# All scale rows before the first projections, head 0's values between the image's and the context's projections

## The chip, the cores and the metric

The kernel runs on one core of a Trainium2 chip. What counts is the device time of one execution in microseconds (us). Each core has TensorE (PE in the rows: matmuls), VectorE (DVE), ScalarE (ACT), GpSimd (POOL) and SyncE (SP, which here issues the loads). Each engine runs its instructions in the order in which the program hands them over, and waits where an instruction needs something of another engine.

## The reference, cut to what matters

One layer of a hybrid block: an adaptive norm, one input projection that feeds a retention mixer (4 heads) and an RG-LRU, their merge, and then an expert layer. The opening, with which this case deals, computes this:

```python
mod_x = silu(c) @ mod_w + mod_b          # shift and scale for the 512 image tokens
mod_c = silu(c_ctx) @ mod_w + mod_b      # the same for the 256 context tokens
hx = rms_norm(x, norm1_g) * (1 + scale_x) + shift_x
hc = rms_norm(ctx, norm1_g) * (1 + scale_c) + shift_c
px, pc = hx @ w_in, hc @ w_in            # parts: q, k, v (retention), gate, u, g (RG-LRU), ...
ux = short_conv(u_x); uc = short_conv(u_c)
r, i = sigmoid(ux @ wa + ba), sigmoid(ux @ wx + bx)   # RG-LRU gates, blocks of 128 channels
h[t] = a[t] * h[t-1] + sqrt(1 - a[t]**2) * i[t] * u[t]  # scan over tokens, both directions; a from r
```

A head of the retention takes scores q k^T with a decay mask, times v, context tokens first; v of a head has 256 columns.

## The kernel before

Everything is kept with the 1024 channels in 8 tiles (KT) of 128 partitions, the tokens along the free axis: 512 of the image (NX), 256 of the context (NC_), 768 together (NT). float32 products are made of three matmuls (mm3, lines 64 to 67): each operand is split into a high part h and a low part l (split, lines 60 to 62: ScalarE copies the high part, VectorE subtracts to get the low one), and hi x hi, hi x lo and lo x hi are added.

The opening: SP loads the inputs. VectorE and ScalarE sum the squares of xT (the image, inv_rms, lines 174 to 186); a matmul with ones spreads the sum (ps_ss), a VectorE instruction scales it and adds epsilon, ScalarE takes the root, VectorE the reciprocal (rstd). Shift and scale of channel tile k come in one of two ways: for k < 4 (NROW) by matmuls, "mod rows" (mod_rows1, lines 198 to 207: 16 matmul instructions on TensorE for image and context at once, a copy by ScalarE, two transposes, two small VectorE instructions); for k of 4 to 7 by two dot products on VectorE for the image (s=0) and two for the context (s=1) (mod_dots, lines 210 to 216). normed (lines 218 to 223) then makes hh and hl (image) or ch and cl (context) of one tile: VectorE, ScalarE, VectorE. The weights of the mod rows (mw, 1 MB each) have two buffers, those of the dot products (mwc, 1 MB each) four; projection weights (w, 512 KB) are loaded in the order of the list plan, two buffers for the loads and four for the split tiles.

The loop over KORD = (0, 4, 1, 2, 5, 6, 3, 7) brings one tile after another: mod rows 2 and 3 or the dot products, normed, then the tile's part of four projections into the PSUM tiles pu, p5, pk and pq (outs0). The context's dot products, norm and projections (into columns 512 to 767 of pu and pk) are written behind it.

Then the loop over four heads. For each: lru_in makes the convolved u from pu (ScalarE copy u, line 303, then six VectorE taps, line 310; split into uh and ul) and the gelu g5 from p5; head computes masks, ropes of k and q, the values v (a PSUM tile pv for two of six token tiles, 24 matmuls for each token tile; vm is the mean, vh and vl the split), then for six tiles scores pS, the masked product P (split to Ph and Pl) and po. lru_scan makes the four gates pg by matmuls from uh and ul (line 65 to 67, 24 in all), then ScalarE and VectorE steps (roots, gi, a, q) and scans (lines 353 to 357). A head has two LRU blocks c = 2h and 2h + 1; the second one's pu and p5 are projected in between.

PSUM has three buffers of 1024 columns (pu, pk, pg, po ..., tag ps2) and two of 512 (p5, pq, pS, pv, tag ps1). In which order each engine gets the instructions around there is set by a scheduler that lists them by its own estimate of when each could run. So the order in the code is not the order on the engines.

Of the kernel before, what the change touches and what calls it, by code (L numbers as in the profile page):

```python
# [17 lines left out]
OP = mybir.AluOpType  # L18
# [34 lines left out]
def block_kernel(ctx: ExitStack, tc: tile.TileContext, A):  # L53
# [10 lines left out]
    def mm3(out, wh, wl, xh, xl, start, stop):  # L64
        PE.matmul(out, wh, xh, start=start, stop=False)  # L65
        PE.matmul(out, wh, xl, start=False, stop=False)  # L66
        PE.matmul(out, wl, xh, start=False, stop=stop)  # L67
# [64 lines left out]
    for j, nm in enumerate(("c", "c_ctx")):  # L132
        S.activation(scol[:, :, j], col(nm, 0, 8), AF.Tanh, scale=0.5)
        V.tensor_scalar(scol[:, :, j], scol[:, :, j], 1.0, 0.5, op0=OP.add, op1=OP.mult)
        V.tensor_tensor(scol[:, :, j], scol[:, :, j], col(nm, 0, 8), op=OP.mult)
    mod1 = const.tile([128, KT, 2, 2], F32, name="mod1")
# [35 lines left out]
    rstd = st.tile([128, NT], F32, name="rstd")  # L172

    def inv_rms(src, o, n):
        ps = psum(n if n == NX else D, name="ps_ss")
        ssq = st.tile([128, NX], F32, name="ssq")
        S.activation(ssq[:, :n], src[:, 0], AF.Square)
        for k in range(1, KT):
            sq = st.tile([128, NX], F32, name="sq", bufs=2)
# [38 lines left out]
    def normed(src, n, s, k, h_, l_):  # L218
        xn = st.tile([128, NX], F32, name="xn", bufs=2)
# [3 lines left out]
        V.scalar_tensor_tensor(l_[:, k], xn[:, :n], shift, f(h_[:, k]), op0=OP.add, op1=OP.subtract)  # L223
# [21 lines left out]
    spin = const.tile([128, 24], F32, name="spin")  # L245
# [808 lines left out]
```

## Time and profile before

| | us |
|---|---|
| median of 3 runs | 1880.65 (1879.25 to 1881.04) |
| profiled execution | 1879.51 |
| its span in the trace | 1877.7 |
| first projection matmul starts | 30.50 |
| last image projection, first matmul behind it | 67.19 |
| first gate matmul | 82.53 |
| first score matmul pS | 115.31 |

In the rows a timeline line is: start, duration, engine, line of the kernel, operation, output <- inputs, shape, count; in brackets the engine's idle time just before and what ended it. Matmuls overlap, so the distance of two starts, not the duration, is what one costs. In a table by stage each engine has its busy time and, in brackets, its instructions. PEclk is the TensorE clock that was granted: 1.00 is 2.4 GHz, 0.50 is 1.2 GHz.

### The profile page before, as it was taken

The numbers are of one execution on the slowest core, as the hardware profiler recorded it, in microseconds if no ns is written. First come the engines' busy times: TensorE is split into PE (matmuls) and PEld (weight loads), VectorE is DVE, ScalarE is ACT, GpSimd is POOL, SyncE is SP. The second block draws the span as 40 slices with busy tenths as digits, with TensorE's granted clock in tenths as the row PEclk, the third lists the DMA queues.
The fourth block names the chain that finished last, engine by engine and source line by source line (L and its number), as shares of the span: only waits on it lengthen the run. The fifth ranks groups of instructions, "written<-read, shape, count | busy, mean of one in ns | idle before, by whom it ended". The sixth has DMA issues, their size and how long they took to land.

```text
span 1877.7 us, 26999 instructions
## 1 busy us (share of the span) xinstructions
PE 1820.2 (97%) x9969; PEld 1603.0 (85%) x9969; DVE 1512.3 (81%) x2801; ACT 824.3 (44%) x1213; POOL 375.7 (20%) x327
## 2 busy tenths in 40 slices
PE   7899999999999999999999999999999999999997
PEld 3788888887888989999999988888887888888885
DVE  8987878788844579999988578886786879788688
ACT  4667575765222444445545333333333333333333
POOL 0000000000000000000022134443443535445350
PEclk9999999999999999999999999999999999999999
DMA  7122121225943433567778999998989999999986
GB/s 310 52 67 68 57 68 57 68 64 189 335 136 115 138 108 115 184 193 238 261 283 299 317 345 328 345 336 298 323 324 312 346 340 337 347 331 355 319 302 208
DMA packets 175753, 432.72 MB, mean 230 GB/s; under 512 B 14082, under 2 KB 87170, under 8 KB 171140
## 3 DMA queue, kind: packets, MB, share of 16 engines
q1 hardware_dynamic: 138756, 296.75, 46.7%
q0 software_dynamic: 36864, 134.23, 19.7%
q8 instruction: 78, 1.28, 0.3%
q14 instruction: 55, 0.45, 0.1%
HBM read 389.32 MB, written 41.62 MB: 229 GB/s over the span
## 4 chain that ended last, share of the span: by engine, by line
PE 74%; DVE 11%; DMA 9%; ACT 3%; issue 2%; SPq 1%; DVEq 0%; ACTq 0%
PE po L65 8%; PE po L66 8%; PE po L67 8%; PE pS L65 7%; PE pS L66 7%; PE pS L67 7%; DMA wt<-wd 4%; DMA vw<-in_v_dram 2%; DVE wl L62 2%; PE pgm L65 1%; PE pgm L66 1%; PE pgm L67 1%; PE pmm L66 1%; PE pmm L67 1%; PE pmm L65 1%
## 5 line engine op out<-in xcount | busy, mean ns | idle before, releaser
L61 ACT ACTIVATE wh<-w 128x1024 fp32r<-128x1024 f32 (+1 forms) x216 | 224.8, 1043 | 369.0 <-DMA w<-in_uT_dram 105.0
L65 PE MATMUL pS<-h2h,wh 128*128 128x384 f32 x1024 | 347.1, 339 | 7.0 <-ACT gt L756 6.7
L67 PE MATMUL pS<-h2h,wl 128*128 128x384 f32 x1024 | 346.1, 338 | 0.7 <-DVE wl L62 0.7
L66 PE MATMUL pS<-h2l,wh 128*128 128x384 f32 x1024 | 346.2, 338 | 0.0
L62 DVE TENSOR_TENSOR wl<-w,wh 128x1024 fp32r<-128x1024 f32 (+1 forms) x216 | 259.0, 1200 | 88.2 <-ACT wh L61 87.5
L801 POOL DMA_INDIRECT row<-in_u_dram,ei x128 | 181.9, 1421 | 609.7 <-DVE row L803 316.0
L66 PE MATMUL po<-vwl,ah 128*128 128x512 f32 x768 | 299.9, 391 | 1.2 <-DVE vwl L62 1.2
L67 PE MATMUL po<-vwh,al 128*128 128x512 f32 x768 | 298.9, 390 | 0.0
L65 PE MATMUL po<-vwh,ah 128*128 128x512 f32 x768 | 271.5, 395 | 10.0 <-ACT vwh L61 8.1
L61 ACT ACTIVATE ah<-af 128x384 fp32r<-128x384 f32 x128 | 67.2, 525 | 387.0 <-PE po L66 220.2
L809 POOL DMA_INDIRECT row<-in_v_dram,ei x128 | 183.9, 1436 | 208.5 <-DVE acc L814 175.2
L65 PEld LDWEIGHTS pS<-h2h,wh 128*128 128x128 f32 x1024 | 193.2, 189 | 14.3 <-ACT gt L756 8.4
L67 PEld LDWEIGHTS pS<-h2h,wl 128*128 128x128 f32 x1024 | 193.1, 189 | 6.0 <-DVE wl L62 1.0
L66 PEld LDWEIGHTS pS<-h2l,wh 128*128 128x128 f32 x1024 | 193.3, 189 | 4.3
L62 DVE TENSOR_TENSOR vwl<-vw,vwh 128x1024 fp32r<-128x1024 f32 x128 | 156.1, 1220 | 27.1 <-ACT vwh L61 25.6
L65 PEld LDWEIGHTS po<-vwh,ah 128*128 128x128 f32 x768 | 143.1, 188 | 38.4 <-ACT vwh L61 10.6
L814 DVE SCALAR_TENSOR_TENSOR acc<-row,act,acc 128x1024 f32<-128x1024 f32 x127 | 162.7, 1281 | 14.0 <-DMA row<-in_v_dram,ei 13.4
L66 PEld LDWEIGHTS po<-vwl,ah 128*128 128x128 f32 x768 | 144.4, 188 | 29.9 <-DVE vwl L62 2.3
L67 PEld LDWEIGHTS po<-vwh,al 128*128 128x128 f32 x768 | 144.4, 188 | 27.8 <-DVE al L62 0.2
L61 ACT ACTIVATE vwh<-vw 128x1024 fp32r<-128x1024 f32 x128 | 134.4, 1051 | 61.6 <-DMA vw<-in_v_dram 59.9
L803 DVE SCALAR_TENSOR_TENSOR row<-row,h2t 128x1024 f32<-128x1024 f32 x128 | 153.8, 1220 | 2.4 <-DMA row<-in_u_dram,ei 2.4
L62 DVE TENSOR_TENSOR al<-af,ah 128x384 fp32r<-128x384 f32 x128 | 71.0, 554 | 62.6 <-ACT ah L61 57.5
(372 smaller groups left out, 3505.8 us busy)
## 6 DMA issues: line engine op xcount, KB each, us to landing
w<-in_uT_dram SPq DMA_DIRECT2D x128, 512.0 KB
vw<-in_v_dram SPq DMA_DIRECT2D x128, 512.0 KB
w<-in_w_in_dram SPq DMA_DIRECT2D x48, 512.0 KB
wd<-stg SPq DMA_DIRECT2D x24, 1024.0 KB
modb<-in_mod_t_dram SPq DMA_DIRECT2D x32, 512.0 KB
wt<-wd SPq DMA_DIRECT2D x9, 1536.0 KB
gd<-gt SPq DMA_DIRECT2D x57, 192.0 KB
gr<-gd SPq DMA_DIRECT2D x57, 192.0 KB
```

The costliest lines, as they stand in the source:

```text
L61: S.activation(hi, src, AF.Copy)
L62: V.tensor_tensor(lo, src, f(hi), op=OP.subtract)
L65: PE.matmul(out, wh, xh, start=start, stop=False)
L66: PE.matmul(out, wh, xl, start=False, stop=False)
L67: PE.matmul(out, wl, xh, start=False, stop=stop)
L801: G.indirect_dma_start(out=row, out_offset=None, in_=A["u"], in_offset=bass.IndirectOffsetOnAxis(ap=ei[:, j:j + 1], axis=0))
L803: V.scalar_tensor_tensor(row, row, 1.0, h2t, op0=OP.mult, op1=OP.mult, accum_out=act[:, j:j + 1])
L809: G.indirect_dma_start(out=row, out_offset=None, in_=A["v"], in_offset=bass.IndirectOffsetOnAxis(ap=ei[:, j:j + 1], axis=0))
L814: V.scalar_tensor_tensor(acc, row, act[:, j:j + 1], acc, op0=OP.mult, op1=OP.add)
```

## The change

The softplus constants (spin, sp and what follows) are written ahead of mod1 and c2, so ahead of the norm. The root is taken by ScalarE straight from PSUM. All four mod rows are written ahead of the projections (issue_after holds the projections back until the last row's transpose), in parts of the PSUM tiles that are used later: halves of pv0, and the free columns of pk and pu. The tiles are taken in the order 0 to 7, tiles 4 and 5 have their dot products before. The value weights of head 0 are loaded early. Behind the image's projections stand the image's values of head 0 (token tiles 0 to 3, into pv0), then the context's part: dot products, norm, projections, and its two value tiles into columns 768 to 1023 of pk and pu. In head(h) only heads 1 to 3 compute their values there; head 0 reads them from pv0 and pvc. In head 0 the step that splits the values stands before lru_scan.

```diff
@@ plan of the weight loads
-                 A["w_v"][h, :, 0:4], A["w_v"][h, :, 4:8], A["w_in"][17 + c], A["w_in"][25 + c], A["gate_w"][c + 1],
+                 *([A["w_v"][h, :, 0:4], A["w_v"][h, :, 4:8]] if h else []),
+                 A["w_in"][17 + c], A["w_in"][25 + c], A["gate_w"][c + 1],
...
@@ block_kernel, inv_rms and the opening
-    def inv_rms(src, o, n):
-        ps = psum(n if n == NX else D, name="ps_ss")
+    def inv_rms(src, o, ps):
+        n = src.shape[2]
...
-        PE.matmul(ps[:, :n], onesf, ssq[:, :n], start=True, stop=True)
-        r = rstd[:, o:o + n]
-        V.tensor_scalar(r, ps[:, :n], 1.0 / D, EPS, op0=OP.mult, op1=OP.add)
-        S.activation(r, r, AF.Sqrt)
-        V.reciprocal(r, r)
+        PE.matmul(ps, onesf, ssq[:, :n], start=True, stop=True)
+        S.activation(rstd[:, o:o + n], ps, AF.Sqrt, scale=1.0 / D, bias=epsc)
+        V.reciprocal(rstd[:, o:o + n], rstd[:, o:o + n])
...
-    inv_rms(xT, 0, NX)
-    KORD = (0, 4, 1, 2, 5, 6, 3, 7)
-    mws = {0: mod_load(0)}
-    prefetch(2)
-    prefetch(4)
-    for k in KORD[1:]:
-        mws[k] = mod_load(k)
-    first = [ahead.pop(0) for _ in range(4)]
-    for k in range(2):
-        mod_rows1(k, mws[k], psum(name="pr"))
-    outs0 = [psum(n, name=nm) for nm, n in (("pu", NT), ("p5", NX), ("pk", NT), ("pq", NX))]
-    for k in KORD:
-        if 1 < k < NROW:
-            mod_rows1(k, mws[k], psum(D, name="pr"))
-        elif k >= NROW:
-            mod_dots(k, mws[k], 0)
-        normed(xT, NX, 0, k, hh, hl)
-        for out, (wh, wl) in zip(outs0, first):
-            mm3(out[:, :NX], wh[:, k], wl[:, k], hh[:, k], hl[:, k], k == KORD[0], k == KORD[-1])
...
-    for k in range(NROW, KT):
-        mod_dots(k, mws[k], 1)
+    outs0 = [psum(n, name=nm) for nm, n in (("pu", NT), ("p5", NX), ("pk", NT), ("pq", NX))]
+    pv0 = psum(D, name="pv0")
+    inv_rms(xT, 0, outs0[1])
+    KORD = tuple(range(KT))
+    mws = {}
+    for k in (0, 4, 1, 5):
+        mws[k] = mod_load(k)
+    prefetch(2)
+    prs = pv0[:, :512], pv0[:, 512:], outs0[2][:, 512:], outs0[0][:, 512:]
+    for k in range(2):
+        mod_rows1(k, mws[k], prs[k])
+    for k in (2, 3, 6):
+        mws[k] = mod_load(k)
+    prefetch(4)
+    mws[7] = mod_load(7)
+    for k in (2, 3):
+        rows = mod_rows1(k, mws[k], prs[k])
     SY.dma_start(cT, A["cT"])
-    inv_rms(cT, NX, NC_)
-    for k in range(KT):
-        normed(cT, NC_, 1, k, ch, cl)
+    first = [ahead.pop(0) for _ in range(4)]
+    wv0 = []
+    for i in range(2):
+        w = wst.tile([128, 4, 256], F32, name="w", tag="w")
+        SY.dma_start(w, A["w_v"][0, :, 4 * i:4 * i + 4])
+        wv0.append([st.tile([128, 4, 256], F32R, name=f"wv{m}", bufs=2) for m in "hl"])
+        split(*wv0[i], w)
+    for k in (4, 5):
+        mod_dots(k, mws[k], 0)
+    with tc.issue_after(rows.ins):
+        for k in KORD:
+            if k > 5:
+                mod_dots(k, mws[k], 0)
+            x_done = normed(xT, NX, 0, k, hh, hl)
+            for out, (wh, wl) in zip(outs0, first):
+                mm = mm3(out[:, :NX], wh[:, k], wl[:, k], hh[:, k], hl[:, k], k == KORD[0], k == KORD[-1])
+
+    def values(out, t, wv):
+        th, tl, o = (hh, hl, 128 * t) if t < 4 else (ch, cl, 128 * t - NX)
+        for k in range(KT):
+            mm = mm3(out, th[:, k, o:o + 128], tl[:, k, o:o + 128], wv[k // 4][0][:, k % 4], wv[k // 4][1][:, k % 4], k == 0, k == KT - 1)
+        return mm
+
+    with tc.issue_after(x_done.ins):
+        inv_rms(cT, NX, outs0[0][:, NT:])
+
+    for t in range(4):
+        with tc.issue_after(mm.ins):
+            mm = values(pv0[:, 256 * t:256 * t + 256], t, wv0)
+    with tc.issue_after(x_done.ins):
+        for k in KORD:
+            if k >= NROW:
+                mod_dots(k, mws[k], 1)
+            normed(cT, NC_, 1, k, ch, cl)
+            for i in (0, 2):
+                wh, wl = first[i]
+                mm = mm3(outs0[i][:, NX:NT], wh[:, k], wl[:, k], ch[:, k], cl[:, k], k == 0, k == KT - 1)
+    pvc = [outs0[i][:, NT:] for i in (2, 0)]
+    for t in (4, 5):
+        with tc.issue_after(mm.ins):
+            mm = values(pvc[t - 4], t, wv0)
...
@@ head(h)
-        wv = [wtile() for i in range(2)]
+        wv = [wtile() for i in range(2)] if h else None
...
@@ loop over heads
             if h == 0:
                 pu, pp, pk, pq = outs0
-                proj_ctx(pu, *first[0])
                 li = lru_in(0, pu, pp)
-                proj_ctx(pk, *first[2])
...
             hd.send((pk, pq))
+            if h == 0:
+                next(hd)
             lru_scan(2 * h, *li)
-            next(hd)
+            if h:
+                next(hd)
```

The queue of loads on SP at the start, kernel before (mw are the tiles of the mod rows, in order 0 to 3; xT the image; m_116 the context cT):

```order
L171 DMA xT<-in_xT_dram 128x2048 x2
L192 DMA mw<-in_mod_a_dram 128x2048
L86 DMA w<-in_w_in_dram 128x1024 x2
L195 DMA mwc<-in_mod_c_dram 128x2048
L192 DMA mw<-in_mod_a_dram 128x2048
L195 DMA mwc<-in_mod_c_dram 128x2048 x3
L247 DMA spin<-in_rd_dram 128x8
L281 DMA m_116<-in_cT_dram 128x2048
L86 DMA w<-in_w_in_dram 128x1024 x2
L192 DMA mw<-in_mod_a_dram 128x2048 x2
```

The same queue in the changed kernel (m_161 is the context):

```order
L204 DMA xT<-in_xT_dram 128x2048 x2
L225 DMA mw<-in_mod_a_dram 128x2048
L228 DMA mwc<-in_mod_c_dram 128x2048
L225 DMA mw<-in_mod_a_dram 128x2048
L228 DMA mwc<-in_mod_c_dram 128x2048
L86 DMA w<-in_w_in_dram 128x1024 x2
L228 DMA mwc<-in_mod_c_dram 128x2048 x2
L275 DMA m_161<-in_cT_dram 128x2048
L225 DMA mw<-in_mod_a_dram 128x2048 x2
L86 DMA w<-in_w_in_dram 128x1024 x2
```

The third and fourth mod tile now stand before the second pair of projection weights, but still behind ten megabytes of other loads.

VectorE between the split of u and the second value tile's low part, kernel before (vm is the value tiles' mean, vl their low part, ul the low part of u, rt and kl the rope of k, sc a mask):

```order
L421 TENSOR_REDUCE vm<-pv 128x2
L389 TENSOR_TENSOR dt_566<-dt_566,dt_567 128x128
L422 TENSOR_SCALAR vm<-vm 128x2
L62 TENSOR_TENSOR ul<-u,uh 128x768
L397 TENSOR_TENSOR sc<-sc,dt_575 128x320
L426 SCALAR_TENSOR_TENSOR vl<-pv,vm,vh 128x256
L397 TENSOR_TENSOR sc<-sc,dt_581 128x320
L367 TENSOR_TENSOR rt<-rx,ssin 64x512 x2
L62 TENSOR_TENSOR kl<-pk,kh 128x256
L426 SCALAR_TENSOR_TENSOR vl<-pv,vm,vh 128x256
```

VectorE at the same place in the changed kernel, from the split of u to the low part of token tile 3 (pv_180 is pv0):

```order
L62 TENSOR_TENSOR ul<-u,uh 128x768
L457 TENSOR_REDUCE vm<-pu 128x1
L458 TENSOR_SCALAR vm<-vm 128x2
L353 SCALAR_TENSOR_TENSOR g_798<-g_798,x_796 128x512
L62 TENSOR_TENSOR wl<-w,wh 128x1024
L429 TENSOR_TENSOR sc<-sc,dt_772 128x320
L462 SCALAR_TENSOR_TENSOR vl<-pv_180,vm,vh 128x256
L429 TENSOR_TENSOR sc<-sc,dt_778 128x320
L399 TENSOR_TENSOR rt<-rx,ssin 64x512 x2
L62 TENSOR_TENSOR kl<-pk,kh 128x256
L457 TENSOR_REDUCE vm<-pk 128x1
L462 SCALAR_TENSOR_TENSOR vl<-pv_180,vm,vh 128x256
```

The low parts of tiles 2 and 3 now stand in the place of those of tiles 0 and 1, which have moved ahead of ul, between the taps.

VectorE behind the first scores, kernel before (P is the masked score, Pl its low part, ul the split of the second LRU block's u):

```order
L437 TENSOR_TENSOR P<-pS,sx 128x512
L62 TENSOR_TENSOR wl<-w,wh 128x1024
L62 TENSOR_TENSOR ul<-u,uh 128x768
L437 TENSOR_TENSOR P<-pS,sx 128x512
L318 TENSOR_SCALAR g_1036<-g_1036 128x512
L62 TENSOR_TENSOR Pl<-P,Ph 128x512
```

VectorE there in the changed kernel (gi<-a,gi are scans of the first LRU block, u taps of the second):

```order
L473 TENSOR_TENSOR P<-pS,sx 128x512
L385 SCALAR_TENSOR_TENSOR gi<-a,gi 128x256
L473 TENSOR_TENSOR P<-pS,sx 128x512
L62 TENSOR_TENSOR wl<-w,wh 128x1024
L389 SCALAR_TENSOR_TENSOR gi<-a,gi 128x768
L342 SCALAR_TENSOR_TENSOR u<-pu,cols,u 128x510
L342 SCALAR_TENSOR_TENSOR u<-pu,cols,u 128x254
L386 SCALAR_TENSOR_TENSOR gi<-a,gi 128x512
L62 TENSOR_TENSOR Pl<-P,Ph 128x512 x2
```

The scans and the first taps now stand between the first P and its low part.

## Rows read from the trace of the kernel before

**Rows 1.** The page, part 1: busy time, share of the span, instructions.

```profile
PE 1820.2 (97%) x9969; PEld 1603.0 (85%) x9969; DVE 1512.3 (81%) x2801; ACT 824.3 (44%) x1213; POOL 375.7 (20%) x327
```

**Rows 2.** Table by stage: stretch, length, busy time of each engine, clock, DMA.

```profile
30.50:67.19 36.69, 34.09 (x134) 22.88 (x135) 35.91 (x98) 16.46 (x30) 0.00 (x0) 0.91 0.25 96
...
79.60:90.00 10.40, 7.58 (x26) 5.89 (x26) 9.45 (x20) 8.61 (x15) 0.80 (x2) 0.67 0.09 25
...
115.30:135.00 19.70, 18.85 (x87) 14.97 (x86) 15.57 (x22) 18.72 (x24) 0.00 (x0) 1.00 0.18 54
135.00:200.00 65.00, 65.00 (x382) 57.49 (x381) 50.42 (x68) 37.03 (x51) 1.81 (x4) 1.00 0.15 49
```

**Rows 3.** Timeline of TensorE, start to the second half of the projections.

```profile
16.36 9.15 PE L200 MATMUL pr<-mw,scol 128*2 128x256 f32 x32
...
25.98 0.28 PE L204 MATMUL pr<-ident,row 2*128 2x2 f32 x2 [0.25 <-ACT row L202]
30.50 0.52 PE L65 MATMUL pu<-hh,wh 128*128 128x512 f32 x1 [4.24 <-ACT hh L222]
...
35.01 0.63 PE L66 MATMUL pu<-hl,wh 128*128 128x512 f32 x1
...
39.56 3.62 PE L200 MATMUL pr<-mw,scol 128*2 128x256 f32 x16
```

**Rows 4.** Timeline of TensorE, from the first gate to the first score.

```profile
82.53 1.22 PE L65 MATMUL pg<-uh,wh 128*128 128x512 f32 x2 [2.82 <-ACT uh L61]
...
89.99 0.28 PE L65 MATMUL pv<-wh,hh 128*128 128x256 f32 x1
...
101.50 0.40 PE L65 MATMUL pu<-hh,wh 128*128 128x512 f32 x1
...
109.84 0.40 PE L65 MATMUL p<-hh,wh 128*128 128x512 f32 x1
...
115.31 0.39 PE L65 MATMUL pS<-qh,kh 128*128 128x512 f32 x1
```

**Rows 5.** DMA from 0 to 36 us: GB/s in 40 slices, then the sum.

```profile
GB/s 0 3 165 100 373 382 419 428 419 428 428 419 391 428 451 423 437 419 428 419 419 437 428 391 437 428 419 419 357 120 301 374 378 410 442 437 441 423 410 428
DMA packets 2390, 13.37 MB, mean 371 GB/s; under 512 B 384, under 2 KB 512, under 8 KB 1026
```

**Rows 6.** Timeline of VectorE: one dot product of 16.

```profile
24.02 1.22 DVE L214 SCALAR_TENSOR_TENSOR mscr<-mwc,m 128x1024 f32<-128x1024 f32 x1
```

**Rows 7.** Timeline of ScalarE: the copy u.

```profile
74.38 0.98 ACT L303 ACTIVATE u<-pu,cols 128x768 f32<-128x768 f32 x1
```

**Rows 8.** Timeline of VectorE, from the taps to the second vl.

```profile
75.13 0.42 DVE L318 TENSOR_SCALAR g<-g 128x512 f32<-128x512 f32 x1
75.46 1.13 DVE L310 SCALAR_TENSOR_TENSOR u<-pu,cols,u 128x510 f32<-128x510 f32 x2
...
81.46 0.68 DVE L421 TENSOR_REDUCE vm<-pv 128x2 f32<-128x512 f32 x1
...
84.93 0.49 DVE L397 TENSOR_TENSOR sc<-sc,dt 128x320 f32<-128x320 f32 x1 [0.66 <-ACT sc L396]
...
87.22 0.47 DVE L426 SCALAR_TENSOR_TENSOR vl<-pv,vm,vh 128x256 fp32r<-128x256 f32 x1
```

**Rows 9.** Timeline of VectorE: scans of the first LRU block, first scores.

```profile
104.08 0.68 DVE L353 TENSOR_TENSOR_SCAN gi<-a,gi 128x256 f32<-128x256 f32 x1
...
105.79 1.75 DVE L357 TENSOR_TENSOR_SCAN gi<-a,gi 128x768 f32<-128x768 f32 x1
...
107.51 1.28 DVE L354 TENSOR_TENSOR_SCAN gi<-a,gi 128x512 f32<-128x512 f32 x1
...
116.19 0.69 DVE L437 TENSOR_TENSOR P<-pS,sx 128x512 f32<-128x512 f32 x1 [0.80 <-PE pS L67]
116.80 1.22 DVE L62 TENSOR_TENSOR wl<-w,wh 128x1024 fp32r<-128x1024 f32 x1
...
119.73 0.69 DVE L62 TENSOR_TENSOR Pl<-P,Ph 128x512 fp32r<-128x512 f32 x1
```

More of the change, by code (lines that the diff above doesn't have):

```diff
@@ L66, in mm3 @@
         PE.matmul(out, wh, xl, start=False, stop=False)
-        PE.matmul(out, wl, xh, start=False, stop=stop)
+        return PE.matmul(out, wl, xh, start=False, stop=stop)
     const = ctx.enter_context(tc.tile_pool(name="const", bufs=1, reuse_waits="tile"))
@@ L135, in block_kernel @@
         V.tensor_tensor(scol[:, :, j], scol[:, :, j], col(nm, 0, 8), op=OP.mult)
+    spin = const.tile([128, 24], F32, name="spin")
+    V.tensor_copy(spin[:, 0:16], col("lam", 0, 16))
+    SY.dma_start(spin[:, 16:24], A["rd"].to_broadcast([128, 8]))
+    sp = const.tile([128, 24], F32, name="sp")
+    sp_w = const.tile([128, 24], F32, name="sp_w")
+    sp_z = const.tile([128, 24], F32, name="sp_z")
+    sp_q = const.tile([128, 24], F32, name="sp_q")
+    S.activation(sp_w, spin, AF.Abs)
+    S.activation(sp_w, sp_w, AF.Exp, scale=-1.0)
+    V.tensor_scalar(sp_z, sp_w, 2.0, None, op0=OP.add)
+    V.reciprocal(sp_z, sp_z)
+    V.tensor_tensor(sp_z, sp_z, sp_w, op=OP.mult)
+    V.tensor_tensor(sp_q, sp_z, sp_z, op=OP.mult)
+    V.memset(sp, 1.0 / 19)
+    for n in range(8, -1, -1):
+        V.tensor_tensor(sp, sp, sp_q, op=OP.mult)
+        V.tensor_scalar(sp, sp, 1.0 / (2 * n + 1), None, op0=OP.add)
+    V.scalar_tensor_tensor(sp, sp, 2.0, sp_z, op0=OP.mult, op1=OP.mult)
+    V.tensor_scalar(sp_w, spin, -1.0, 0.0, op0=OP.mult, op1=OP.max)
+    V.tensor_tensor(sp, sp, sp_w, op=OP.add)
+    sp4 = const.tile([128, 16], F32, name="sp4")
+    V.tensor_scalar(sp4, sp[:, 0:16], 4.0, None, op0=OP.mult)
+    nsp4 = const.tile([128, 16], F32, name="nsp4")
+    V.tensor_scalar(nsp4, sp[:, 0:16], -4.0, None, op0=OP.mult)
+    hb = const.tile([128, 32], F32, name="hb")
+    V.tensor_scalar(hb, col("ba", 0, 32), 0.5, None, op0=OP.mult)
+    lgam = const.tile([128, 8], F32, name="lgam")
+    V.tensor_scalar(lgam, sp[:, 16:24], -1.0, None, op0=OP.mult)
+    nlgam = sp[:, 16:24]
+    lg768 = const.tile([128, 4], F32, name="lg768")
+    V.tensor_scalar(lg768, lgam[:, 4:8], 768.0, None, op0=OP.mult)
     mod1 = const.tile([128, KT, 2, 2], F32, name="mod1")
@@ L172, in block_kernel @@
     rstd = st.tile([128, NT], F32, name="rstd")
-    def inv_rms(src, o, n):
-        ps = psum(n if n == NX else D, name="ps_ss")
+    epsc = const.tile([128, 1], F32, name="epsc")
+    V.memset(epsc, EPS)
+    def inv_rms(src, o, ps):
+        n = src.shape[2]
         ssq = st.tile([128, NX], F32, name="ssq")
@@ L218, in normed @@
     def normed(src, n, s, k, h_, l_):
-        xn = st.tile([128, NX], F32, name="xn", bufs=2)
+        xn = st.tile([128, NX], F32, name="xn", tag="xn", bufs=2)
         shift = mod1[:, k, 0, s:s + 1]
@@ L410, in head @@
         vl = rp.tile([128, 6, 256], F32R, name="vl")
[L411 removed]
+        wv = [wtile() for i in range(2)] if h else None
         for t2 in range(3):
[L413 to L421 removed]
+            if h:
+                pv = psum(name="pv")
+                for tt in range(2):
+                    values(pv[:, 256 * tt:256 * tt + 256], 2 * t2 + tt, wv)
+                pv = pv.rearrange("p (a b) -> p a b", a=2)
+            elif t2 < 2:
+                pv = pv0[:, 512 * t2:512 * t2 + 512].rearrange("p (a b) -> p a b", a=2)
+            vm = rp.tile([128, 2], F32, name="vm", bufs=2)
+            if h or t2 < 2:
+                V.tensor_reduce(vm, pv, axis=AX.X, op=OP.add)
+            else:
+                for tt in range(2):
+                    V.tensor_reduce(vm[:, tt:tt + 1], pvc[tt], axis=AX.X, op=OP.add)
             V.tensor_scalar(vm, vm, -1.0 / 256, None, op0=OP.mult)
             for tt in range(2):
[L424 removed]
+                t, src = 2 * t2 + tt, pv[:, tt] if h or t2 < 2 else pvc[tt]
                 S.activation(vh[:, t], src, AF.Identity, bias=vm[:, tt:tt + 1])
```

49 lines of the change are left out of this document (4 added, 45 removed).

## The prediction

> **What bounds the kernel now.** I read the page first: TensorE is busy in 97% of the span [rows 1], so nearly every microsecond that it stands still or runs at half clock in the opening is a microsecond of the kernel. Then the table by stage [rows 2]. From 30.50 to 67.19 us, the image projections, VectorE is busy for 35.91 of 36.69 us and sets the pace. From 79.60 to 90.00, the first gates, TensorE works for 7.58 of 10.40 us at a mean granted clock of 0.67. From 115.30 to 135.00 it loses 0.85 us, and from 135.00 to 200.00 nothing at all (65.00 of 65.00). So what is lost before 135 is not earned back behind it. Then the timelines: TensorE's rows show two idle times after which matmuls run at half rate, 4.24 us before the first projection and 2.82 us before the first gate [rows 3, 4]. A clock of 1.2 GHz in place of 2.4 costs there what the gates show: 24 matmuls from 82.53 to 89.99, 7.46 us, where twelve of 0.23 and twelve of 0.12 would be 4.2. A drop costs some 3.2 us.
>
> The sum below goes along TensorE to three points: the first projection (30.50 before), the end of the image projections (67.19), and the first score matmul pS (115.31). The fourth term is what happens just behind pS.
>
> **The change part by part: the mod rows.** All four rows now stand ahead of every projection. The first two use weight tiles that have long landed. The third and fourth do not: their tiles share two buffers with the first two, so their loads are issued only when the rows before have been computed, behind all that the queue already holds. In before, 13.37 MB had moved by 36.0 us at a steady 0.42 MB/us [rows 5]. Counted by the sizes of the loads, the third tile's last byte is number 12.68 million there, so it came at about 34.4. In the change two weight tiles (1.05 MB) go behind it, so 2.5 us earlier: 31.9. It didn't matter in before, where that row was computed at 39.56, in the middle of the projections. Now TensorE has nothing between the second row's end (25.5 in before, hardly another time now) and 31.9. That idle time is longer than the 4.24, so I let the third row run at half clock: 2 x 3.62 = 7.24, to 39.1. The fourth at full clock: 3.62, to 42.8. Copy and transposes take 0.8 (25.51 to 26.26) [rows 3]: the first projection starts at 43.6, 13.1 us later than before.
>
> **The image projections.** VectorE is freed of eight dot products of 1.22 us [rows 6], the context's sum of squares and the softplus chain, which go behind or into its early idle time. The normed tiles are ready long before TensorE wants them, and 96 matmuls run at the pitch of the projection at 109.84 to 115.31 (24 in 5.47, 0.228) [rows 4]: 21.9, to 65.5. That is 1.7 before the old 67.19. The fewer table loads and the two VectorE instructions saved on the root lie beside TensorE's wait for the tile and are worth nothing.
>
> **Values and context.** 96 value matmuls for the image, 48 for the context's projections, 48 for its values, each 0.12 (96 from 89.99 to 101.50 [rows 4]): 23.0, and 0.5 for the sum of squares. The context's normed tiles are made under the 11.5 us of image values. So TensorE goes through without a wait to 89.0. In before the same work lay partly behind the gates; so far the change is ahead, since only the gates (4.2 at full clock) and the next projections are left to pS.
>
> **What then waits.** Tile 5's values were put into the free columns of pu, and u, the copy from which the gates' input is made, reads that tile. The built order lets u wait for the last of these matmuls, at 89.0, though its own columns were complete 5.8 us before. u takes 0.98 on ScalarE [rows 7]. And the gates need the big PSUM buffers, of which the values hold pv0, pk and pu: the first gate waits until VectorE has read tile 3 for the last time (vl). In VectorE's new order that stands behind all taps, the gelu, the split of u, a weight split and the ropes. The same list, in before, runs from the first tap at 75.46 to the second vl's end at 87.69: 12.2 us, of which 0.66 idle [rows 8]. The new list has one g more (0.42), two more vl (0.47 each) and two reductions of a single tile (not above the double one's 0.68): 14.1 at most, less the idle and 0.08 of overlap for each neighbour; I take 13.4. The gates start at 89.0 + 0.98 + 13.4 = 103.4. TensorE has only the second input projection p5 (24 matmuls, 5.47) for this time, to about 96.1, and then idles over 7 us. The gates again at half clock, 7.46: 110.9. Then pu, which in before ran ahead, 8.34 (101.50 to 109.84): pS at 119.2, against 115.31. **+3.9 us.** Bounds: +1.5 if the tile lands 2.5 us earlier than counted, +6 if later by as much.
>
> Here a rule speaks against the change too. The Trainium skill, in "PSUM — Partial Sum Buffer", section "PSUM bank collisions raise a hardware error", asks that engines be kept apart by bank, not by address; columns 512 to 1023 of pu are one bank, with the context's part that u reads and tile 5's values. By that rule the wait of u could not be dropped by a finer guard; without it the sum would be 5.8 smaller. No row of before shows two engines in one bank.
>
> **Behind pS.** In before the scans of the first LRU block are over before pS. Now gates come some 20 us later, and their scans fall into the score stage. On VectorE a scan (0.68), a second P (0.69), a weight split (1.22), the long scan (1.75), two taps (1.13) and another scan (1.28) stand between the first P and its low part Pl [rows 8, 9]: 6.75 less six overlaps, 6.3 us, where before Pl came 2.85 us behind P's end (116.88 to 119.73). P ends 1.6 behind pS, so Pl ends 8.6 behind pS. TensorE has 13 matmuls of 0.23 before it needs Pl, and with its small waits is through at about 3.7: it stands for 4.9 us, and pays another 3.1 at half clock. Less the 0.85 lost here before, with 0.35 for the other waits: **+7.5 us.** Bounds: 0, if the scans turn out not to lie in the way, and 9.
>
> Sum: 3.9 + 7.5 = 11.4 on the profiled execution's 1879.51: 1890.9. The median of the runs lies 1.1 above that execution; I keep 1891, since the wait behind pS may be partly covered.
>
> **Rivals.** *The gates don't wait for the values' last readers* (faster). Then they follow u as before, 8.15 us behind its start (74.38 to 82.53 [rows 4, 7]): 89.0 + 8.15 = 97.2. TensorE waits 1.1 after p5, keeps its clock, is through the gates at 101.4 and at pS at 109.7, 5.6 us early; the scans are then out of the way as well, and the result is -4 to -6: 1875 to 1877. It decides from the point where vl of tile 3 ends before p5 does (96.1), so VectorE would have to be 7 us faster. For it: TensorE's work itself is in fact more tightly packed up to 89.0. Against it: VectorE was full in the same list before [rows 8]. Chance 0.20.
>
> *Only the first loss comes* (about the same): what VectorE does between P and Pl has been finished under pu's 8.34 us. +3.9, 1883.4 to 1884.5, on the edge of what can be told. Against it: the gates' q and roots must come from ScalarE first. Chance 0.15.
>
> *u isn't held by the values in its tile* (a smaller loss): everything from u to pS 5.8 earlier, pS at 113.4, the stall behind it as forecast: 11.4 - 5.8 = 5.6, 1885 to 1886. Chance 0.05. By the skill's rule named above it shouldn't happen.
>
> *The forecast*, 1886 to 1896: 0.60.
>
> **How the numbers follow.** A measurement of this kernel can tell about 0.2% (3.8 us) from no change. Faster: the first rival's part beyond 3.8 us, 0.17. Same: its rest and half of the second, 0.14. Slower: the other half, the third, the forecast and what lies beyond it, 0.69. The range leaves out some 0.1 on either side: from 1876, which takes in most of the first rival, to 1896, where both upper bounds (6 + 9 on 1879.5, 1894.5) are reached.
>
> **What would show it.** In the trace of the changed kernel: an idle time of 6 to 8 us on TensorE ended by the third mod row, with its 16 matmuls taking about 7 us; first projection at 42 to 45; image projections at 0.228 each without waits, ending at 64 to 67; no idle time from there to 88 to 90; u starting right behind the last value matmul; an idle time of 6 to 8 us before the first gate, ended by vl; pS at 117 to 120; and an idle time of 4 to 6 us before a matmul on Pl. The forecast is wrong if the gates start before 98 or if no wait over 2 us stands behind pS.

## The result and the profile after

The changed kernel takes 1890.94 us (median of 13 runs, 1882.50 to 1894.78), the kernel before 1879.42 (13 runs beside it). The ratio of the two is 1.0059, with a 95% interval of 1.0043 to 1.0074: slower by 8 to 14 us. The forecast was 1891.0, and slower. The profiled execution took 1887.92 us, its span 1886.2, against 1879.51 and 1877.7.

TensorE does the same work: 9969 matmuls, busy for 1818.7 us by the page, where [rows 1] have 1820.2. So the loss is, over the whole span, time in which TensorE stands still. The table by stage tells where. Its columns are the stretch, its length, the busy time of PE, PEld, DVE, ACT and POOL with their instructions, the granted clock, the DMA share and GB/s. First the kernel before, then the changed one, over the same stretches:

```profile
15.00:44.00 29.00, 23.67 (x80) 11.24 (x79) 27.79 (x55) 11.78 (x21) 0.00 (x0) 0.88 0.82 324
44.00:88.00 44.00, 38.93 (x205) 30.75 (x204) 40.28 (x105) 25.08 (x42) 1.81 (x4) 0.93 0.18 58
88.00:118.00 30.00, 29.27 (x187) 26.49 (x186) 26.69 (x40) 19.95 (x27) 0.00 (x0) 0.99 0.22 70
118.00:136.00 18.00, 17.88 (x84) 14.48 (x83) 13.94 (x21) 17.02 (x22) 0.00 (x0) 1.00 0.19 59
```

```profile
15.00:44.00 29.00, 21.45 (x82) 8.32 (x81) 23.95 (x50) 10.89 (x16) 0.00 (x0) 0.88 0.85 339
44.00:88.00 44.00, 43.74 (x284) 40.01 (x282) 34.27 (x66) 15.53 (x28) 0.45 (x1) 1.00 0.20 63
88.00:118.00 30.00, 21.04 (x98) 17.83 (x99) 23.99 (x43) 25.86 (x39) 1.36 (x3) 0.83 0.18 55
118.00:136.00 18.00, 12.28 (x42) 8.63 (x41) 17.94 (x27) 6.76 (x11) 0.00 (x0) 0.81 0.09 29
```

Take busy from length. From 15 to 44 us TensorE stands for 7.55 us where it stood for 5.33: 2.2 lost. From 44 to 88 it stands for 0.26 instead of 5.07: 4.8 won, and this is the change doing what it says, a row of projections, values and context without a gap. From 88 to 118 it stands for 8.96 instead of 0.73: 8.2 lost. From 118 to 136 it stands for 5.72 instead of 0.12: 5.6 lost. The four make 11.2 lost in all. That is a measure of the places, not the loss itself: matmuls at half clock count as busy, and the same stretch holds other work in the two kernels. The last score matmul of the last head starts at 405.5 in before and at 415.2 here, 9.7 later; the span ends 8.5 later. From here on that score matmul is the yardstick, one value from one trace for each version. Runs of one kernel lie several us apart (the kernel before from 1873.78 to 1886.68), and part of that arises behind it: two versions with it at 405.5 and 406.0 had spans of 1877.7 and 1873.4. Ahead of it, four versions with the same opening start their projections within 0.33 us of each other (42.10 to 42.43), the versions with the loads in another order within 1.5 (34.11 to 35.59). So a difference of 1 us on the yardstick can't be told from chance. The row that gives it groups one line and one tile, with the starts of the first and the last:

```profile
L65 PE MATMUL pS<-qh,kh x24: 388/395/504, 117.6 to 415.2; 128*128 128x512 f32 x24
```

Now the waits, in the timeline of TensorE (start, duration, engine, line, operation; in brackets the idle time before it and what ended it). They answer to [rows 3, 4]:

```profile
32.78 5.26 PE L233 MATMUL pk<-mw,scol 128*2 128x256 f32 x16 [6.45 <-DMA mw<-in_mod_a_dram]
37.88 3.62 PE L233 MATMUL pu<-mw,scol 128*2 128x256 f32 x16
...
42.23 0.50 PE L65 MATMUL p<-hh,wh 128*128 128x512 f32 x1
...
87.46 0.28 PE L67 MATMUL pu<-wvh,cl 128*128 128x256 f32 x1
89.31 0.50 PE L65 MATMUL p<-hh,wh 128*128 128x512 f32 x1 [1.57 <-ACT x L347]
...
102.70 0.77 PE L65 MATMUL pg<-uh,wh 128*128 128x512 f32 x1 [7.65 <-DVE vl L462]
...
109.31 0.39 PE L65 MATMUL pu<-hh,wh 128*128 128x512 f32 x1
...
117.63 0.40 PE L65 MATMUL pS<-qh,kh 128*128 128x512 f32 x1
...
120.54 0.50 PE L65 MATMUL pS<-qh,kh 128*128 128x512 f32 x1 [1.00 <-DVE P L473]
...
127.33 0.80 PE L66 MATMUL po<-Pl,vh 128*128 128x512 f32 x1 [4.64 <-DVE Pl L62]
```

Three waits, each with its name: 6.45 us for the third mod tile, 7.65 for VectorE's vl before the first gate, 4.64 for VectorE's low part Pl of the first probabilities. ScalarE's copy u, from which the gates' input is made, starts right behind the last value matmul, though nothing of its own columns was missing:

```profile
87.78 0.99 ACT L335 ACTIVATE u<-pu,cols 128x768 f32<-128x768 f32 x1 [4.54 <-PE pu L67]
```

What the first gate waits for is a buffer and not its input. ScalarE has made uh at 94.85 and VectorE ul at 96.63; the last reading of pv0, the low part of token tile 3, ends at 102.55, and the gates start at 102.70. One line of ScalarE's timeline, then two of VectorE's:

```profile
94.00 0.85 ACT L61 ACTIVATE uh<-u 128x768 fp32r<-128x768 f32 x1 [1.06 <-DVE u L342]
```

```profile
95.68 0.95 DVE L62 TENSOR_TENSOR ul<-u,uh 128x768 fp32r<-128x768 f32 x1
...
102.08 0.47 DVE L462 SCALAR_TENSOR_TENSOR vl<-pv,vm,vh 128x256 fp32r<-128x256 f32 x1
```

And behind the first scores VectorE has the scans of the first LRU block between P and Pl, where in [rows 9] they were over:

```profile
119.81 0.68 DVE L473 TENSOR_TENSOR P<-pS,sx 128x512 f32<-128x512 f32 x1
120.41 0.68 DVE L385 TENSOR_TENSOR_SCAN gi<-a,gi 128x256 f32<-128x256 f32 x1
121.00 0.66 DVE L473 TENSOR_TENSOR P<-pS,sx 128x512 f32<-128x512 f32 x1
121.59 1.21 DVE L62 TENSOR_TENSOR wl<-w,wh 128x1024 fp32r<-128x1024 f32 x1
122.72 1.75 DVE L389 TENSOR_TENSOR_SCAN gi<-a,gi 128x768 f32<-128x768 f32 x1
124.39 1.11 DVE L342 SCALAR_TENSOR_TENSOR u<-pu,cols,u 128x510 f32<-128x510 f32 x2
125.42 1.27 DVE L386 TENSOR_TENSOR_SCAN gi<-a,gi 128x512 f32<-128x512 f32 x1
126.61 1.26 DVE L62 TENSOR_TENSOR Pl<-P,Ph 128x512 fp32r<-128x512 f32 x2
```

### The profile page after: what moved, and what is told of

Read it like the earlier page. It is cut to its first block, busy times and chain, and to the rows that moved or that the text cites. A ratio compares the mean times of both kernels' runs of the same rounds, so it can differ in the third digit from the quotient of the medians.

```text
span 1886.2 us, 26991 instructions
## 1 busy us (share of the span) xinstructions
PE 1818.7 (96%) x9969; PEld 1602.1 (85%) x9969; DVE 1512.3 (80%) x2800; ACT 823.0 (44%) x1211; POOL 377.7 (20%) x327
## 4 chain that ended last, share of the span: by engine, by line
PE 74%; DMA 11%; DVE 7%; ACT 3%; issue 3%; SPq 2%; POOL 1%; DVEq 0%; ACTq 0%; POOLq 0%
PE pS L65 7%; PE pS L66 7%; PE pS L67 7%; PE po L65 7%; PE po L66 7%; PE po L67 7%; DMA wt<-wd 4%; DMA vw<-in_v_dram 3%; DMA row<-in_v_dram,ei 2%; PE pgm L65 1%; PE pgm L66 1%; PE pgm L67 1%; PE pmm L66 1%; PE pmm L67 1%; PE pmm L65 1%
## 5 line engine op out<-in xcount | busy, mean ns | idle before, releaser
L838 POOL DMA_INDIRECT row<-in_u_dram,ei x128 | 187.5, 1464 | 598.1 <-DVE row L840 305.1
```

What stands on the lines that cost most here:

```text
L838: G.indirect_dma_start(out=row, out_offset=None, in_=A["u"], in_offset=bass.IndirectOffsetOnAxis(ap=ei[:, j:j + 1], axis=0))
```

## The experiments

The theory was that of the prediction: three waits, each with a cause of its own (the order of the loads, the buffer that u shares, the scans ahead of Pl). Rivals: that one cause carries the others (a late start that is handed on), that VectorE is full in any order, or that the half clock is the price and not the waits. "Last pS" is the yardstick named above: 405.5 in before, 415.2 in the changed kernel.

### Half of the change: the rows alone

All four mod rows ahead of the projections; the values stay in the head, as before.

```diff
-    pv0 = psum(D, name="pv0")
+    pr0 = psum(D, name="pr")
...
-    for t in range(4):
-        with tc.issue_after(mm.ins):
-            mm = values(pv0[:, 256 * t:256 * t + 256], t, wv0)
-    pvc = [outs0[i][:, NT:] for i in (2, 0)]
-    for t in (4, 5): ...
...
```

> The changed kernel with all values of head 0 left where the kernel before has them (in the head, with its own tile pv), so only the mod rows, the tile order, the early softplus and the context's part behind the image stand as changed. My theory: most of the loss comes with the rows, since TensorE waits for the third row's tile until about 32.8 us and starts to project at about 42, and without values there is nothing to put between the image's and the context's projections, so TensorE waits there some 5 us for the context's norm. Expected against the kernel before: +5 to +8 us at the last head's scores (405.5 us in before), 1885 to 1888. Rival: the loss comes with the moved values (u held, gates held), and the rows alone are worth the 1.5 to 2.5 us by which the image projections end earlier: -2 us.

Measured: 1.0041 [1.0021, 1.0061], last pS 410.2. The rows alone lose 4.7 us, just short of the 5 to 8 expected, so the early values lose the other 5.0: theory and rival have about half each. The wait for the third tile is here too, 6.04, and the context, whose wait was to be filled by values, stops TensorE for 4.53. The first gate waits 2.91 us, and what ends it is its input uh, not a buffer:

```profile
32.87 3.57 PE L232 MATMUL pk<-mw,scol 128*2 128x256 f32 x8 [6.04 <-DMA mw<-in_mod_a_dram]
...
69.75 0.58 PE L65 MATMUL pu<-ch,wh 128*128 128x256 f32 x1 [4.53 <-ACT ch L254]
...
88.36 1.22 PE L65 MATMUL pg<-uh,wh 128*128 128x512 f32 x2 [2.91 <-ACT uh L61]
```

### The first wait: which loads stand ahead of the third tile

The last pair of column tiles and the context are issued behind the fourth mod tile, 3 MB that stood ahead of it. First in the changed kernel:

```diff
-            SY.dma_start(mw, A["mod_a"][k])
+            dmas[k] = SY.dma_start(mw, A["mod_a"][k])
...
-    for k in (2, 3, 6):
+    for k in (2, 3):
         mws[k] = mod_load(k)
     prefetch(4)
-    mws[7] = mod_load(7)
+    with tc.issue_after(dmas[3].ins):
+        for k in (6, 7):
+            mws[k] = mod_load(k)
...
-    SY.dma_start(cT, A["cT"])
+    with tc.issue_after(dmas[3].ins):
+        SY.dma_start(cT, A["cT"])
```

> The changed kernel with the loads of dot tiles 6 and 7 and of the context (3 MB) issued behind the fourth mod row's load. Theory: the third row waits for its tile because of what stands ahead of it in the queue; its tile then lands soon after it can be issued (the first row ends at 20.4), at about 25 to 27, the idle time of 6.45 us goes below 2, and the first projection starts at 34 to 38 in place of 42.2. Part of that is eaten by VectorE's normed tiles; the last head's scores come 5 to 7 us earlier than in the changed kernel (415.2). Rival: the projections are bound by VectorE or by the projection weights, which also stand behind the fourth row's load: the image projections end where they did (65), gain under 1.5 us.

Measured: 1.0034 [1.0018, 1.0049], last pS 410.5, 4.7 earlier than in the changed kernel, where 5 to 7 were expected. The wait for the third tile is gone, the one that is left stands before the fourth and is 0.80, and the third and fourth rows both run at full rate (3.62 and 3.61). The first projection starts at 34.11, 8.1 earlier. Half of this is lost on the way: the image projections take 23.96 us where they took 21.90, since VectorE's low part and ScalarE's weight split now hold them, and the stretch from there to p5 takes 27.16 where it took 25.18. The gates start 4.1 earlier. The two later waits have kept their lengths to a hundredth:

```profile
29.77 3.61 PE L234 MATMUL pu<-mw,scol 128*2 128x256 f32 x16 [0.80 <-DMA mw<-in_mod_a_dram]
...
38.26 0.50 PE L66 MATMUL pu<-hl,wh 128*128 128x512 f32 x1 [0.66 <-DVE hl L257]
...
40.70 0.50 PE L65 MATMUL pk<-hh,wh 128*128 128x512 f32 x1 [0.79 <-ACT wh L61]
...
98.62 0.77 PE L65 MATMUL pg<-uh,wh 128*128 128x512 f32 x1 [7.65 <-DVE vl L466]
...
123.17 0.79 PE L66 MATMUL po<-Pl,vh 128*128 128x512 f32 x1 [4.64 <-DVE Pl L62]
```

So the late start doesn't cause the two later waits: they are the same length wherever they lie.

The same order of loads with the rows alone:

> The kernel with the values left in the head (as rows_first_only) and the 3 MB of loads behind the fourth row's. Theory: the rows cost 4.7 us at the last head's scores (410.2 against 405.5) only because the third row's tile lands late; with the loads turned round this is won back: 403.5 to 406.5, so the kernel within 2 us of the one before. Rival: what is won before the image projections is lost again in the wait of 4.53 us for the context's norm, which starts from VectorE's end of the image's tiles: 408.5 or more.

Measured: 1.0003 [0.9983, 1.0023], last pS 406.0. The rows ahead of the projections, as such, cost nothing and give nothing that can be told (the interval runs from -3 to +4 us); the 4.7 us of the rows alone were the order of the loads. What is won is lost in the context's waits, 1.41 and 4.38 us:

```profile
61.26 0.70 PE L216 MATMUL pu<-ssq,onesf 128*128 128x256 f32 x2 [1.41 <-DVE ssq L215]
66.33 0.58 PE L65 MATMUL pu<-ch,wh 128*128 128x256 f32 x1 [4.38 <-ACT ch L255]
```

### The second wait: the tile that u reads

Tiles 4 and 5 of the values change places: tile 4 goes into pu's free columns, tile 5 into pk's.

```diff
-    pvc = [outs0[i][:, NT:] for i in (2, 0)]
+    pvc = [outs0[i][:, NT:] for i in (0, 2)]
```

> The changed kernel with the two context value tiles exchanged: tile 4 goes into pu first, tile 5 into pk behind it. So u may start 24 matmuls of 0.12 us (2.9 us) earlier, at about 84.9 in place of 87.8. Theory: u and the VectorE list behind it set the first gate, so gate, first pS and the last head's scores come 2.5 to 3 us earlier than in the changed kernel (102.70, 117.63 and 415.2 there): the kernel 7 us slower than before in place of 9.7. Rival: the copy isn't held by the tile, or VectorE's list is bound elsewhere: no shift of the gate, under 0.5 us.

Measured: 1.0054 [1.0034, 1.0074], last pS 411.8, 3.4 earlier. u starts at 84.77, 3.0 earlier than 87.78, which is one tile of values (24 matmuls of 0.12), and the gates start 3.0 earlier too:

```profile
84.77 0.99 ACT L335 ACTIVATE u<-pu,cols 128x768 f32<-128x768 f32 x1 [1.66 <-PE pu L67]
```

```profile
99.70 0.77 PE L65 MATMUL pg<-uh,wh 128*128 128x512 f32 x1 [6.62 <-DVE vl L462]
```

That u is held by the last matmul into its tile is shown by this: the two tiles' places are all that was changed. It is shown by the traces; by the medians alone this version (1.0054) is not to be told from the changed kernel (1.0059). The Trainium skill's rule, in "PSUM — Partial Sum Buffer", section "PSUM bank collisions raise a hardware error", to guard by bank, agrees with how the kernel behaves; a kernel that lets u read beside a matmul in the same bank was not tried, since it would break that rule.

Both edits together:

> Both edits: the 3 MB behind the fourth row's load, and the value tiles exchanged. Theory: the two waits lie one behind the other on one chain, so the gains add: the last head's scores 8 to 10 us earlier than in the changed kernel (415.2), so 0 to 2 us from the kernel before. Rival: a common bound behind both (the wait of the first low part Pl of 4.64 us grows by what is won): under 6 us.

Measured: 1.0030 [1.0012, 1.0047], last pS 409.4: 5.8 earlier than in the changed kernel where 8 to 10 were expected. In this execution the fourth mod row starts at 31.06, 1.29 later than with the loads alone (29.77); counted from there the first score comes 2.5 earlier than with the loads alone (111.77 less 31.06, against 113.00 less 29.77), so the exchange is worth nearly its 3 us here too and the sum missed by the start. When the fourth tile is used varies by over a us among the versions that load it in the same way (29.77, 31.06, and 30.28 in the version with all three edits below).

### The third wait: the low part ahead of the scans

In the first head VectorE makes the first Pl before the two scans that have no order of their own against it.

```diff
+                scans.append(V.tensor_tensor_scan(i[:, NX:], ...))
...
+                scans.append(V.tensor_tensor_scan(i[:, ::-1], ...))
...
-            split(Ph, Pl, P)
+            S.activation(Ph, P, AF.Copy)
+            low = V.tensor_tensor(Pl, P, f(Ph), op=OP.subtract)
+            if h == 0 and j < 1:
+                for sc_ in scans[:2]:
+                    tc.add_manual_dep(sc_.ins, low.ins.name, ...)
```

> The changed kernel with the first two scans of LRU block 0 queued on VectorE behind the low part of the first masked score (Pl). Theory: the wait of 4.64 us before the first matmul on Pl comes from what stands between P and Pl on VectorE, scans above all; it goes below 2 us, TensorE keeps its clock there, and the last head's scores come 2 to 4 us earlier than in the changed kernel (415.2). Rival: something else is late at the same time (the scans' results, the second block's taps and gates), so what is won at Pl is lost a few us later: under 1 us.

Measured: 1.0062 [1.0044, 1.0080], last pS 414.0. The wait falls as told, from 4.64 to 1.49, and TensorE keeps its clock: 1.00 from 118 to 136 us, where it was 0.81. But of these 3.2 us and the half clock together only 1.2 us reach the end, short of the 2 to 4 expected and about as much as the yardstick can tell; the median (1.0062 beside the changed kernel's 1.0059) doesn't show it. Behind the wait new ones stand:

```profile
124.00 0.51 PE L66 MATMUL po<-Pl,vh 128*128 128x512 f32 x1 [1.49 <-DVE Pl L479]
126.83 0.51 PE L66 MATMUL po<-Pl,vh 128*128 128x512 f32 x1 [1.16 <-DVE Pl L479]
128.48 0.50 PE L65 MATMUL pS<-qh,kh 128*128 128x512 f32 x1 [0.20 <-DVE P L475]
130.25 0.50 PE L65 MATMUL pS<-qh,kh 128*128 128x512 f32 x1 [0.53 <-DVE P L475]
132.18 0.73 PE L65 MATMUL pg<-uh,wh 128*128 128x512 f32 x2 [0.96 <-ACT uh L61]
```

With the first they are 4.34 us. VectorE is busy here for 17.86 of 18.00 us from 118 to 136, as it was in the changed kernel (17.94), so what stands behind the scans waits instead. That VectorE is full there, the rival, explains more of this loss than the place of the scans.

All three edits together:

> The changed kernel with all three repairs: loads behind, value tiles exchanged, low part of the first masked score ahead of the scans. Theory: the repairs lie on different places of one chain and add, the first two gave 409.4 at the last head's scores, the third 2 to 4 more: 405.5 to 407.5, the same as before within 2 us. Rival: the third gives nothing on top (409 or more), because VectorE as a whole is full from the taps to the scans and any order of it costs the same.

Measured: 1.0020 [1.0005, 1.0034], last pS 407.3, inside the range expected. Of the 9.7 us, 7.9 are undone by three edits that leave the change's plan as it is. For the other 1.8 there is no experiment.

### The clock: work put into the second wait

The second input projection of the first head is computed twice (24 matmuls more, 5.47 us, the same numbers), so that TensorE is busy while it waits for vl.

```diff
-            proj(pp, *wtile())
+            wp = wtile()
+            if h == 0:
+                proj(pp, *wp)
+            proj(pp, *wp)
```

> The changed kernel with the 24 matmuls of the second block's p5 done twice (the second time overwrites the first; the result is the same), so that TensorE works through most of the 7.65 us before the gates. It is 5.5 us more of work. Theory: the gates start no later, at 102 to 103, and run at full clock, 4.2 in place of 6.6 us, as far as their buffers come free in time; the first pS comes 1 to 2.4 us earlier (117.63), and so do the last head's scores (415.2). Rival: the half clock costs nothing there, because the gates wait for each other's PSUM buffers anyway: no shift, or later by up to 1 us.

Measured: 1.0066 [1.0048, 1.0084], last pS 414.9. That 24 matmuls could be added at no cost shows that the wait is VectorE's and not TensorE's. The first pS came at 117.61, where it was 117.63: no shift, as the rival had it. The price of the clock the run doesn't tell: the first gate's six matmuls ran at full rate behind an idle time of 1.51, and then, behind another of 0.99, the clock fell all the same:

```profile
102.19 0.47 PE L65 MATMUL pg<-uh,wh 128*128 128x512 f32 x1 [1.51 <-DVE vl L462]
...
104.48 0.50 PE L65 MATMUL pg<-uh,wh 128*128 128x512 f32 x1 [0.99 <-ACT roots L367]
104.81 0.58 PE L66 MATMUL pg<-ul,wh 128*128 128x512 f32 x1
```

The next projection pu started at 109.28, and at 109.31 without the added work. What half clock alone costs here stays open; behind pS, in the version above, the kept clock and the shorter wait brought 1.2 us together.

### Towards a better kernel: two tiles of values in the context's wait

Rows first, with the loads in the order that costs nothing. Of the values only tiles 0 and 1 are computed early, between the image's and the context's part, in a buffer that u doesn't use; the other four stay in the head, and the first Pl stands ahead of the scans.

```diff
-    for t in range(4):
+    for t in range(2):
         with tc.issue_after(mm.ins):
-            mm = values(pv0[:, 256 * t:256 * t + 256], t, wv0)
+            mm = values(pr0[:, 256 * t:256 * t + 256], t, wv0)
-    pvc = [outs0[i][:, NT:] for i in (2, 0)]
-    for t in (4, 5): ...
...
```

> Rows before the projections with the third pair of column tiles and the context behind the mod tiles, as in rows_first_loads_behind; of the values only image tiles 0 and 1 are computed early, between the image's and the context's part (about 9.2 us of TensorE work in front of waits of 1.41 + 4.38 us there), the other four stay in the head; the low part of the first block of probabilities stands ahead of the scans. My theory (a wait is worth what work that is needed anyway stands in it, and moved values cost only where they bind a buffer or run before their reader needs them): the 1.41 and 4.38 us for the context go and the 2.80 us before the first gate stays, the wait for the first low part falls from about 4.6 to 1.5 us; the last head's pS near 402 (400 to 405) against 405.5 in before and 406.0 in rows_first_loads_behind, ratio 0.996 to 1.000. Rival (what is taken from one wait comes back at the next one, the first vl or the low part): last pS at 406 to 410, ratio 1.000 to 1.003.

Measured: 1878.09 us, 0.9992 [0.9975, 1.0010]; last pS 403.8, 1.7 earlier than in before. It is the fastest of the versions, and not to be told from the kernel before. The expectation for the waits was wrong, and also its count of the work: two tiles are 48 matmuls of 0.12, 5.8 us and not 9.2. They went into the context's waits of 1.41 + 4.38 = 5.8, and 4.0 of these are still there; and the wait before the gates has grown, from 2.80 with the rows and this order of loads to 4.72:

```profile
65.25 0.70 PE L217 MATMUL pu<-ssq,onesf 128*128 128x256 f32 x2 [0.54 <-DVE ssq L216]
69.38 0.58 PE L65 MATMUL pu<-ch,wh 128*128 128x256 f32 x1 [3.43 <-ACT ch L256]
...
87.42 1.22 PE L65 MATMUL pg<-uh,wh 128*128 128x512 f32 x2 [4.72 <-DVE vm L455]
```

In this kernel VectorE's timeline has a single gap over 0.2 us from 54 to 88 (1.26, at 77.7): the last dot products for the context, each of them 1.22, its sum of squares, its norm and four weight splits lie in one row. Work for TensorE can't fill a wait that VectorE lengthens.

So the small operations of VectorE that nobody needs at once were given to GpSimd:

```diff
-            V.tensor_tensor(ssq[:, :n], ssq[:, :n], sq[:, :n], op=OP.add)
+            (V if o == 0 else G).tensor_tensor(ssq[:, :n], ssq[:, :n], sq[:, :n], op=OP.add)
...
+        W = V if c else G
-        V.tensor_scalar(g5, g5, 0.044715, 1.0, op0=OP.mult, op1=OP.add)
+        W.tensor_scalar(g5, g5, 0.044715, 1.0, op0=OP.mult, op1=OP.add)
...
```

> As two_tiles_filled, where VectorE stood without a gap from 54 to 88 us, with VectorE's small operations that nobody needs at once given to GpSimd: the seven adds of the context's sum of squares (0.42 us each, 2.9 us), and in the first block the two of the tanh gate (0.42 and 0.69) and the five of the retention strips (three of 0.28, two of 0.45). My theory (VectorE binds the stretch from the context's norm to the first gate): the waits of 0.54 + 3.43 us for the context and 4.72 us before the first gate, 8.7 us together, fall by 3 to 5 us, and the last head's pS comes at 399 to 402 against 403.8 in two_tiles_filled and 405.5 in before; ratio 0.996 to 0.999. Rival (another thing binds it: ScalarE's order, or GpSimd is so slow that its adds end later than VectorE's): waits of 8 us or more in sum, last pS 403 or later, ratio 0.999 to 1.003.

Measured: 0.9996 [0.9978, 1.0014], last pS 406.6, as the rival had it. The waits are 3.57 us for the sum of squares, 2.53 and 0.90 at the gates, 7.0 against 8.7: less than the 3 to 5 us won that were expected, and less left than the rival's 8. But the first one stands behind the tenth of the 48 value matmuls, since the built order put the sum's matmul there, and what follows the waits runs at half clock. The gates start at 87.16, where they started at 87.42. The run tells that in this order GpSimd's help doesn't bring the gates forward; with another place for that matmul it wasn't tried. First TensorE's timeline, then GpSimd's, then VectorE's in the same stretch:

```profile
64.12 1.22 PE L217 MATMUL pu<-ssq,onesf 128*128 128x256 f32 x2 [3.57 <-POOL ssq L216]
...
87.16 1.45 PE L65 MATMUL pg<-uh,wh 128*128 128x512 f32 x2 [2.53 <-ACT uh L61]
```

```profile
53.66 10.40 POOL L216 TENSOR_TENSOR ssq<-ssq,sq 128x256 f32<-128x256 f32 x6 [0.53 <-ACT sq L215]
```

```profile
56.54 0.58 DVE L249 TENSOR_TENSOR mod<-mod,modb 128x2 f32<-128x2 f32 x1
...
58.19 0.68 DVE L250 SCALAR_TENSOR_TENSOR scal<-mod,cols 128x1 f32<-128x1 f32 x1
...
65.07 0.15 DVE L249 TENSOR_TENSOR mod<-mod,modb 128x2 f32<-128x2 f32 x1
```

Six adds take GpSimd 10.40 us, 1.73 each (the first of the seven, ahead of them, took 0.86), where VectorE took 0.42. And VectorE's own operations on one or two columns take 0.57 to 0.68 as long as GpSimd adds, and 0.15 when it has done (65.07).

No version beats the kernel before by more than its interval.

## Why the prediction was right

The time came out at 1890.94 where 1891.0 was forecast, and the waits came where they were told, each ended by what was named. That the two figures agree to a tenth is luck. Step by step:

- **The third mod tile.** Forecast: idle from 25.5 to 31.9, the row at half clock throughout (7.24), first projection 43.6. Measured: idle for 6.45 to 32.78, the row 5.26, first projection 42.23. The clock came back within the row (the fourth row is 3.62 again), so the term was 2 us too dear; the tile was 0.9 later than counted. The experiment on the loads shows the cause: it is what stands ahead of it in the queue.
- **Image projections.** 21.9 at 0.228 each, as forecast: 42.23 to 64.13, where the first value matmul starts, 1.4 before the 65.5 of the sum, which is the row's difference carried on.
- **Values and context without a wait.** As forecast: 0.26 us idle from 44 to 88; the last value matmul at 87.46, forecast 89.0.
- **u held by the values in its tile, and the gates behind vl.** u at 87.78 and 13.9 us from its end (88.77) to the gates, forecast 13.4 by the list of [rows 8]. The exchange of tiles 4 and 5 shows the first half. The second, that the gates wait for the last reading of pv0, is read from the trace (ul ready at 96.63, vl of tile 3 done at 102.55) and was not tried by itself: no version has all the image's values early in a buffer that the gates don't need. A wait of 1.57 before p5, for ScalarE's copy that frees its buffer, was not foreseen; it cost nothing, since TensorE then waits for vl all the same.
- **The gates.** 6.6 us (102.70 to 109.31), forecast 7.46 after [rows 4]. The clock came back sooner. First pS at 117.6, forecast 119.2; this term is +2.3 and not +3.9, inside its bounds.
- **Behind pS.** Forecast a wait of 4.9 for Pl and 3.1 at half clock. Measured 4.64, and behind it ten matmuls in 4.42 (127.33 to 131.75) where 0.23 each would make 2.3: 2.1. Another 1.00 stands before it for P. Less the 0.85 of before that is 6.9; from the first pS to the last the loss is 9.7 - 2.3 = 7.4, forecast 7.5. The remaining 0.5 lies in no row shown here, and that the two figures meet is chance in part. The place of the scans is also not the whole cause: with two of them moved behind Pl only 1.2 us came back, since VectorE is full there in either order.

The sum of 11.4 was thus 1.7 above the 9.7 of the trace. That the medians are 11.5 apart is chance to that extent: the interval is 8 to 14.

Three slips in the working changed nothing. VectorE is said to set the pace of the image projections in the kernel before; in the same row TensorE is busy for 34.09 of 36.69 us, so it stood for only 2.6 us there. The upper bound of the first term is 6.4 by its own rule (3.9 and 2.5) and not 6. And the chances of the four cases, split as the text says, make 0.105 for same and 0.725 for slower, not 0.14 and 0.69.

The rivals. That the gates don't wait for the values' last readers fell with the 6 us between ul and the first gate. That only the first loss comes fell with the 4.64. That u isn't held fell with u's start at 87.78.

One sentence of the prediction turned out poorer than it sounds: the change is ahead until 89.0. It is, by TensorE's work. But the values that were computed ahead held the buffer that the gates needed, until VectorE's list had come to their last reading, and with the values used up TensorE had only p5 (to 94.9) to put into that time. Where the values stay in the head, in buffers of their own, the first gate waits 2.91 us.

## What to carry to other kernels

Ask of work that is moved into a wait what its result will hold until it is read, and what it covered where it stood: here the values filled 44 to 88 us, and then held the gates' buffer to 102.55, with 7.65 us in which TensorE had nothing to do. Count what is queued ahead of a load that is issued late; 3 MB ahead of one tile were worth 4.7 us, and reordering them gave these back with nothing else changed. Before reordering a full engine's list, add up its busy time in the stretch: VectorE worked for 17.9 of 18.0 us there, and putting Pl first gave 1.2 us. Don't put a result into the spare columns of a tile that a reader on the path still needs, unless it comes before that reader's own columns: one tile of values in pu held u by 3.0 us.

## What the runs showed of the hardware

An idle time need not be long to be followed by half clock: behind 1.51 us the matmuls ran at full rate, and behind 0.99 more, six matmuls later, they fell to half (from 104.81 on; at 108.18 the rate is back). Which of the two idle times brought it about, or both, no run here tells. In the version with the low part first two idle times of much the same length, 1.49 and 1.16 us and also six matmuls apart, were followed by none: the granted clock was 1.00 there.

GpSimd's adds on tiles of 256 columns took four times VectorE's 0.42 beside VectorE's dot products, and VectorE's operations on one or two columns, 0.15 otherwise, took 0.57 to 0.68 meanwhile, while the dot products between them took 1.21 as before (one took 1.64). The Trainium skill, "SBUF — State Buffer", section "SBUF: two separate sides", says that the two engines share a pair of ports that the one locks against the other for a whole instruction, VectorE among other cases when it reads two operands from SBUF. The trace agrees so far as both were slower at once; which instruction waited for which it doesn't show.
